# Row blocks of 2560 bytes and seven weight tiles in a one-core decoder step

## The chip, the cores and the metric

The kernel runs on one core of one Trainium2 chip. The metric is the time of one launch in device microseconds (us), the median of several runs.

## The reference

One layer of a decoder on 256 prompt rows and 32 sample rows (eight sequences of four new tokens), 288 rows in all, width 2048, in float32:

```python
def ffn_half(h, g, wg, wu, wd):
    hn = rms_norm(h, g)
    return h + 0.5 * ((jax.nn.silu(hn @ wg) * (hn @ wu)) @ wd)     # inner width 5632
...
hp = ffn_half(hp, norm_ffn1[l], w_ffn1_gate[l], w_ffn1_up[l], w_ffn1_down[l])
cb, u, q, k, v, logf = mixer_in(hp, norm_mix[l], w_in[l], b_f[l])  # one projection, 2048 -> 6152
conv_y = cb * short_conv(u_ext, conv_w[l])                         # half the mixer: gated 3-tap convolution
attn_o = fox_prompt(q, k, v, logf)                                 # the other half: 8 heads of attention
hp = mixer_out(hp, conv_y, attn_o, norm_conv_out[l], norm_attn_out[l], w_out[l])
hp = ffn_half(hp, norm_ffn2[l], w_ffn2_gate[l], w_ffn2_up[l], w_ffn2_down[l])
hp = ple_add(hp, p_prompt[l], norm_ple[l], w_ple_gate[l], w_ple_proj[l])
y_prompt = rms_norm(hp, norm_final)
```

The sample rows go through the same steps; their attention also reads 1024 past tokens per sequence from paged caches of K and V through a page table.

## The kernel before

Features lie on the partitions and the 288 rows along the free axis. A matrix of width 2048 is 16 row blocks of 128 x 288; `h` is the residual stream in this form.

Every product with a weight matrix is taken in three matmuls of one pass each. The rows and the weights are both split into a high part, rounded to the type float32r, and a low part, the remainder. For each row block and each 128 columns of weights, `pair` (its inner `fn`) issues low rows by high weights, high rows by high weights, and high rows by low weights: the first two on L338, the third on L340. The high weights are `whi`, the low ones `wlo`. The first gate and up pairs (`rows_first`) take high before low.

The row operand of most products is `x`, made from `h` by `split` (ScalarE writes the high part, VectorE the low one, L206 and L207). The inner rows of an FFN are `hid`, written in `up` (L417, L418). Both tiles are laid out by `both`: block k has its high part of 288 float32 (1152 bytes), and right behind it its low part, so a block takes 2304 bytes, nine times 256. An offset ahead of the first block (`BEFORE_X` 55 and `BEFORE_W` 7 elements) sets where the parts stand; with the addresses that the allocator gives these tiles, the high parts stand at 252 and the low ones at 124 modulo 256. `zc` (rows of the convolution) and `ph` (per-layer input) are laid out by `both` as well. The attention rows `zah` and `zal` are tiles of their own, at 224 and 96 modulo 256.

Weights come from memory in tiles of four row blocks by 256 columns (512 KB, tags `raw0` to `raw7`, `RAW` = 8). They are loaded by SP's queue in the order of `items`; `load_upto` runs `state["ahead"]` items ahead of use. A tile is split into `whi` and `wlo` in halves of two blocks (L292; ScalarE, then VectorE), five halves ahead of TensorE. A weight tile is free again when its second half is split. The first eight tiles are loaded at the start in smaller parts, interleaved by hand with the parts of `x` (the list `order`); after them SP's queue has the gains and the constants.

During the mixer the V pages (512 KB each, 64 of them) come by indirect DMAs from POOL's queue. In that part only four weight tiles (`WEIGHTS`) serve weights; `page_tile` gives the pages the other weight tiles, three tiles of their own, and one that held attention scores and comes free last:

```python
own = ([(rawp, f"raw{i}") for i in range(WEIGHTS, RAW)] + [(W["vx"][0], f"v{i}") for i in range(VPAGES)]
       + [(W["mix"][0], "wideb")])
n = state["pages"]
state["pages"] += 1
p, tag = own[n] if n < len(own) - 1 else own[(n + 1) % len(own)]
```

Sixteen rounds (`v_round`, four pages and 16 short matmuls each, L825) are set among the products, a round every two or three steps (`VSTEP` 2.7), where a step is one weight tile's matmuls. There `ahead` is 12 items, weights and pages together. Beside page loads, POOL multiplies and adds (masks, residual adds, sums of squares).

The tile framework schedules the instructions of each engine from the order of the program; what is pinned (`keep_in_program_order`) stays in that order.

Of the kernel before, what the change touches and what calls it, by code (L numbers as in the profile page):

```python
# [17 lines left out]
F32R = mybir.dt.float32r  # L18
# [7 lines left out]
P = 128  # L26
D = 2048
KT = D // P
# [4 lines left out]
NT = SEQ + NS  # L33
# [7 lines left out]
NEG = -1e30  # L41
UE = 2 + SEQ + DB * 6

RAW = 8
HALVES = 5
BEFORE_X = 55
BEFORE_W = 7
MANUAL = False
BANKS = dict(mm=3, kt=3, va=2)
KPAIRS = (1, 8, 14, 21, 27, 34, 40, 47)  # L50
# [44 lines left out]
def build(nc, tc, ctx, A, O):  # L95
    def pool(name, bufs=1, to=ctx, **k):
        return to.enter_context(tc.tile_pool(name=name, bufs=bufs, reuse_waits="tile", **k))

    v, s, g, pe, sy = nc.vector, nc.scalar, nc.gpsimd, nc.tensor, nc.sync

    cst = pool("cst")
    xp = pool("xp")
# [96 lines left out]
    def norm_scale(out, squares, width, chunks, load=False):  # L199

        s.activation(sqh, squares, AF.Copy)
        v.tensor_tensor(sql, squares, sqh.bitcast(F32), ALU.subtract)
        defer(lambda: inv_rms(out, [sqh, sql], width, load), chunks)
# [4 lines left out]

    X = {}

    def both(p, name, blocks, before, **k):
        n = blocks * 2 * NT
        whole = 64 if k else 8
        t = p.tile([P, -(-(before + n) // whole) * whole], F32R, name=name, tag=name, **k)
        t = t[:, before:before + n].rearrange("p (k s n) -> p s k n", s=2, n=NT)
        return t[:, 0], t[:, 1]

    def new_x():
        X["hi"], X["lo"] = both(xp, "x", KT, BEFORE_X)

    def make_x(k, gname, work):

        split(X["hi"][:, k, :], X["lo"][:, k, :], h[:, k, :], gain(gname, k))
        squares(k, work)
# [13 lines left out]
    items = []  # L238
    state = dict(wslot=0, pages=0, through=False, ahead=RAW, loaded=0, split=0, used=0, halves_used=0, chunk=0, lead=HALVES)

    def load_upto(n, parts=None):
        while state["loaded"] < min(n, len(items)):
            it = items[state["loaded"]]
            if it["kind"] == "p" and "vx" not in W:
                return
            if it["kind"] == "w":
                state["wslot"] = (state["wslot"] + 1) % (WEIGHTS if state["pages"] and not state["through"] else RAW)
                t = rawp.tile([P, it["nk"], 256], F32, name="wraw", tag=f"raw{state['wslot']}")
                src = it["src"]
                if parts is not None:  # L250
                    cuts = (0, 1, 2, 3, 4) if state["loaded"] < 2 else (0, 2, 4)
                    parts.append([(t[:, a:b], src[:, a:b]) for a, b in zip(cuts, cuts[1:])])
                else:
                    d = sy.dma_start(t, src)
                    if state["used"] < 24:
                        tc.keep_in_program_order(d)
            else:
                t = page_tile()
                g.indirect_dma_start(out=t, out_offset=None, in_=it["src"],  # L259
                                     in_offset=bass.IndirectOffsetOnAxis(ap=it["rows"], axis=0))  # L260
            it["tile"] = t
            state["loaded"] += 1

    def page_tile():
# [6 lines that stand above are left out]
        return p.tile([P, 9 * P] if tag == "wideb" else [P, NH * P], F32, name="page", tag=tag)[:, :NH * P]  # L271
# [85 lines left out]
    def run_steps():  # L357
        for its, _ in steps:
            items.extend(its)
            for it in its:  # L360
                if it["kind"] == "w":
                    halves.extend((it, j) for j in range(0, it["nk"], 2))
        for i in range(0, 16, 4):
            halves[i + 1], halves[i + 2] = halves[i + 2], halves[i + 1]
        for its, fn in steps:
            load_upto(state["used"] + state["ahead"])
            fn()
            state["used"] += len(its)

    def do(fn):  # L370
        steps.append(([], fn))
# [18 lines left out]
    def ffn(wg, wu, wd, nextgain, work):  # L390
        npairs = DFF // 256
        groups = [range(0, 3), range(3, 6)] + [range(p, p + 4) for p in range(6, npairs, 4)]
        H = {}
        for gi, grp in enumerate(groups):
            firstg = gi == 0 and nextgain == "norm_mix"

            def start():
                H["hi"], H["lo"] = both(work(), "hid", 8, BEFORE_W, bufs=2)
            do(start)
            for pi, pr in enumerate(grp):  # L400
                sg = {}

                def gate(b, o, sg=sg):
                    w = work()
                    t = w.tile([P, NT], F32, name="tg", tag="tg", bufs=2)
                    v.tensor_tensor(t, o, rs, ALU.mult)  # L406
                    u = w.tile([P, NT], F32, name="sg", tag="sg", bufs=2)
                    s.activation(u, t, AF.Silu)  # L408
                    r = w.tile([P, NT], F32, name="sr", tag="sr", bufs=3)
                    g.tensor_tensor(r, u, rs, ALU.mult)  # L410
                    sg[b] = r

                def up(b, o, sg=sg, pi=pi):
                    t = work().tile([P, NT], F32, name="hd", tag="hd", bufs=2)
                    v.tensor_tensor(t, o, sg[b], ALU.mult)  # L415
                    k = 2 * pi + b
                    s.activation(H["hi"][:, k, :], t, AF.Copy)  # L417
                    v.tensor_tensor(H["lo"][:, k, :], t, H["hi"][:, k, :].bitcast(F32), ALU.subtract)  # L418

                lead = firstg and pi == 0  # L420
                gs = pair(wg, pr * 256, list(range(KT)), xact, gate, **(dict(late=4 if lead else 2, tag="va", rows_first=lead) if pr == 0 else {}))
                us = pair(wu, pr * 256, list(range(KT)), xact, up, **(dict(late=4, tag="kt", rows_first=True) if lead else {}))
                steps.extend([x for gu in zip(gs, us) for x in gu] if lead else gs + us)
            k0 = grp[0] * 2
            nb = 2 * len(grp)
            lastg = gi == len(groups) - 1
            for ob in range(KT // 2):
                def down(b, o, ob=ob, lastg=lastg):
                    k = 2 * ob + b
                    v.scalar_tensor_tensor(h[:, k, :], o, 0.5, h[:, k, :], ALU.mult, ALU.add)  # L430
                    if lastg:
                        if k == 0:
                            new_x()
                        make_x(k, nextgain, work())
                steps.extend(pair(wd, ob * 256, list(range(k0, k0 + nb)),
                                  lambda k: (H["hi"][:, k, :], H["lo"][:, k, :]), down, k_of=lambda k, k0=k0: k - k0))
        do(lambda: norm_scale(rs, acc, D, 3, True))
# [11 lines left out]
    def x_load(a, b, e=sy):  # L449
        c = slice(KT + a * NT if a else 0, KT + b * NT)  # L450
        tc.keep_in_program_order(e.dma_start(hx[:, c], A["x"][:, c]))
# [67 lines left out]
    for its, _ in steps[2:34]:  # L519
        items.extend(its)  # L520
    first_in = []
    load_upto(8, first_in)
    order = [(0, 1), (s, 0), (sy, 1), (s, 0), (1, 2), (sy, 1), (sy, 0), (sy, 1), (sy, 0), (sy, 1)]
    for a in (2, 3):
        x_load(a, a + 1, g)
    order += [(4, 6), (sy, 2), (sy, 3), (6, 8), (sy, 2), (sy, 3)]
    for a in (4, 6):
        order += [(2 * a, 2 * a + 2), (sy, a), (sy, a + 1), (2 * a + 2, 2 * a + 4), (sy, a), (sy, a + 1)]
    for where, what in order:
        if isinstance(where, int):  # L530
            x_load(where, what)
        else:
            tc.keep_in_program_order(where.dma_start(*first_in[what].pop(0)))
# [388 lines left out]
    def state_in():  # L922
        M["st"] = W["zq"][0].tile([P, CB, DB, 2], F32, name="st")
        M["zc"] = both(W["zq"][0], "zc", CB, BEFORE_W)
        g.dma_start(M["st"].rearrange("p i b t -> p i (b t)"), A["state"])
# [168 lines left out]
    def mix_end():  # L1094
        norm_scale(rs, acc, D, 3)
        state["ahead"] = RAW
        for n in ("vx", "vp", "vv", "cv", "mix", "zq", "tq"):
# [12 lines left out]
    def ple_start():  # L1110
# [4 lines left out]
        g.dma_start(pa, A["p"])  # L1115
        E["hi"], E["lo"] = both(w, "ph", 2, BEFORE_W)
        for k in range(2):
# [61 lines left out]
    do(finish)  # L1179
    with (tc.manual_schedule(engines={mybir.EngineType.PE}) if MANUAL else ExitStack()):  # L1180
        run_steps()
# [67 lines left out]
```

## Time and profile before

| | |
|---|---|
| median of 3 runs | 2266.62 us (2265.76 to 2267.56) |
| the profiled execution's own time | 2266.11 us |
| its span, first to last instruction | 2264.3 us |
| granted TensorE clock | 0.998 |
| TensorE matmul busy | 2250.4 us (99%) |
| VectorE, ScalarE, POOL busy | 1342.5, 1047.3, 323.0 us |
| read from memory | 435.41 MB |

In rows of the profile, "out<-in" names the tiles, the "x" number counts instructions, and what stands behind the bar is busy time, mean ns of one instruction, and idle time of the engine ahead of them with what ended it. In a timeline a row has its start, its length (both in us), the engine and the operation; rows that follow one another with the same names are merged, "x2" being two. In a table of stretches, each row has the stretch, its length, the busy time of TensorE, its weight loads, VectorE, ScalarE and POOL with their counts, the granted clock, the share of time in which the DMA engines were busy, and GB/s. A row of waits has the total, the number of waits and the longest.

### The profile page before, as it was taken

What the parts mean: (1) busy time and instruction counts of PE and PEld (TensorE: products, weight loads), DVE (VectorE), ACT (ScalarE), POOL (GpSimd) and SP (SyncE); (2) the same over time, 40 slices, a digit from 0 to 9 for tenths busy, and PEclk for the clock granted to TensorE, in tenths of its full rate; (3) what the DMA queues carried; (4) which work ended last, traced back from release to release, by engine and by line L of the source; (5) the groups of instructions that cost most, each with busy time, mean ns of one, the idle gap of its engine ahead of it and who ended that gap; (6) DMA issues with size and microseconds to landing.
All of it is one profiled execution on the core that took longest, in us unless ns stands there. A gap on an engine that the chain in (4) does not pass through costs nothing.

```text
span 2264.3 us, 44311 instructions
## 1 busy us (share of the span) xinstructions
PE 2250.4 (99%) x17387; PEld 2194.2 (97%) x17387; DVE 1342.5 (59%) x2413; ACT 1047.3 (46%) x1860; POOL 323.0 (14%) x398
## 2 busy tenths in 40 slices
PE   9999999999999999999999999999999999999997
PEld 9999999999999999888888999999999999999997
DVE  7555555555555586456567875555555555555865
ACT  6444444444444553334344554444444444444654
POOL 1020000000000013345446210000000000000210
PEclk9999999999999999999999999999999999999999
DMA  8575555555555556988988555555555555555552
GB/s 278 169 245 169 170 174 168 168 169 171 172 169 168 168 168 238 332 300 302 331 323 301 167 171 159 179 162 182 168 168 168 174 170 170 168 169 172 169 171 94
DMA packets 342865, 443.37 MB, mean 196 GB/s; under 512 B 17424, under 2 KB 307104, under 8 KB 342656
## 3 DMA queue, kind: packets, MB, share of 16 engines
q1 hardware_dynamic: 320944, 366.25, 50.6%
q0 software_dynamic: 20480, 71.67, 8.9%
q8 instruction: 136, 2.23, 0.4%
q10 hardware_dynamic: 1232, 2.62, 0.3%
q14 instruction: 73, 0.60, 0.1%
HBM read 435.41 MB, written 5.07 MB: 195 GB/s over the span
## 4 chain that ended last, share of the span: by engine, by line
PE 99%; DVE 0%; DMA 0%; issue 0%; ACT 0%; DVEq 0%; ACTq 0%
PE mm L338 61%; PE mm L340 30%; PE va L338 2%; PE va L825 1%; PE va L758 1%; PE va L340 1%; DMA KT<-in_cache_k_dram,idx 0%; PE kt L338 0%; DVE h L1175 0%; PE kt L340 0%; PE kt L879 0%; PE kt L912 0%; PE mm L518 0%; PE kt L903 0%; PE kt L878 0%
## 5 line engine op out<-in xcount | busy, mean ns | idle before, releaser
L338 PE MATMUL mm<-x,whi 128*128 128x288 f32 x7360 | 1438.0, 291 | 0.0
L292 DVE TENSOR_TENSOR wlo<-wraw,whi 128x512 fp32r<-128x512 f32 (+1 forms) x1388 | 974.8, 706 | 748.0 <-ACT whi L292 653.2
L292 ACT ACTIVATE whi<-wraw 128x512 fp32r<-128x512 f32 (+1 forms) x1388 | 862.3, 628 | 881.0 <-PE mm L338 776.9
L338 PEld LDWEIGHTS mm<-x,whi 128*128 128x128 f32 x7360 | 1163.2, 187 | 15.9 <-issue 11.8
L340 PE MATMUL mm<-x,wlo 128*128 128x288 f32 x3680 | 1067.2, 290 | 0.1
L340 PEld LDWEIGHTS mm<-x,wlo 128*128 128x128 f32 x3680 | 689.0, 187 | 0.3 <-DVE wlo L292 0.3
L338 PE MATMUL mm<-hid,whi 128*128 128x288 f32 x2816 | 547.9, 291 | 0.0
L338 PEld LDWEIGHTS mm<-hid,whi 128*128 128x128 f32 x2816 | 445.2, 187 | 0.0
L340 PE MATMUL mm<-hid,wlo 128*128 128x288 f32 x1408 | 408.3, 290 | 0.0
L410 POOL TENSOR_TENSOR sr<-sg,rs 128x288 f32<-128x288 f32 x88 | 71.7, 815 | 1392.8 <-ACT sg L408 1392.6
L340 PEld LDWEIGHTS mm<-hid,wlo 128*128 128x128 f32 x1408 | 263.6, 187 | 0.0
L430 DVE SCALAR_TENSOR_TENSOR h<-mm,h 128x288 f32<-128x288 f32 x192 | 85.8, 454 | 20.0 <-PE mm L340 20.0
L408 ACT ACTIVATE sg<-tg 128x288 f32<-128x288 f32 x88 | 39.0, 444 | 97.7 <-DVE tg L406 97.6
L735 POOL DMA_INDIRECT KT<-in_cache_k_dram,idx x64 | 65.1, 1017 | 129.3 <-DVE idx L166 51.8
L417 ACT ACTIVATE hid<-hd 128x288 fp32r<-128x288 f32 x88 | 39.1, 445 | 92.9 <-DVE hd L415 92.9
L232 POOL TENSOR_TENSOR acc<-acc,sq 128x288 f32<-128x288 f32 x52 | 43.9, 845 | 220.8 <-ACT sq L231 218.3
L259 POOL DMA_INDIRECT page<-in_cache_v_dram,idx x64 | 65.2, 1018 | 63.3 <-PE va L825 42.4
L418 DVE TENSOR_TENSOR hid<-hd,hid 128x288 fp32r<-128x288 f32 x88 | 40.1, 457 | 21.9 <-ACT hid L417 21.9
L338 PE MATMUL mm<-zc,whi 128*128 128x288 f32 x256 | 52.0, 297 | 0.0
L338 PE MATMUL va<-x,whi 128*128 128x288 f32 x256 | 51.2, 293 | 0.0
L415 DVE TENSOR_TENSOR hd<-mm,sr 128x288 f32<-128x288 f32 x86 | 39.0, 454 | 17.1 <-PE mm L340 17.1
L406 DVE TENSOR_TENSOR tg<-mm,rs 128x288 f32<-128x288 f32 x84 | 37.8, 450 | 14.6 <-PE mm L340 13.5
(236 smaller groups left out, 1058.7 us busy)
## 6 DMA issues: line engine op xcount, KB each, us to landing
wraw<-in_w_ffn_gate_dram SPq DMA_DIRECT2D x172, 512.0 KB
wraw<-in_w_ffn_up_dram SPq DMA_DIRECT2D x172, 512.0 KB
wraw<-in_w_ffn_down_dram SPq DMA_DIRECT2D x160, 512.0 KB
wraw<-in_w_in_dram SPq DMA_DIRECT2D x96, 512.0 KB
wraw<-in_w_out_dram SPq DMA_DIRECT2D x32, 512.0 KB
wraw<-in_w_ple_gate_dram SPq DMA_DIRECT2D x32, 512.0 KB
wraw<-in_w_ffn_down_dram SPq DMA_DIRECT2D x32, 256.0 KB
wraw<-in_w_ple_proj_dram SPq DMA_DIRECT2D x8, 256.0 KB
```

The source lines that it names most:

```text
L232: (v if k >= KT - last_on_v else g).tensor_tensor(acc, acc, sq, ALU.add)
L259: g.indirect_dma_start(out=t, out_offset=None, in_=it["src"], in_offset=bass.IndirectOffsetOnAxis(ap=it["rows"], axis=0))
L292: for i in s.activation(hi, x, AF.Copy), v.tensor_tensor(lo, x, hi.bitcast(F32), ALU.subtract):
L338: pe.matmul(o, hi[:, j % 2, w], x, start=f, stop=False)
L340: state["product"] = pe.matmul(o, lo[:, j % 2, w], xh, start=False, stop=l)
L408: s.activation(u, t, AF.Silu)
L410: g.tensor_tensor(r, u, rs, ALU.mult)
L415: v.tensor_tensor(t, o, sg[b], ALU.mult)
L417: s.activation(H["hi"][:, k, :], t, AF.Copy)
L418: v.tensor_tensor(H["lo"][:, k, :], t, H["hi"][:, k, :].bitcast(F32), ALU.subtract)
L430: v.scalar_tensor_tensor(h[:, k, :], o, 0.5, h[:, k, :], ALU.mult, ALU.add)
L735: d = g.indirect_dma_start(out=t[:, i].rearrange("p h s -> p (h s)"), out_offset=None, in_=A["cache_k"], in_offset=bass.IndirectOffsetOnAx ...
```

## The change

A row block of `x` and of `hid` takes 640 elements (2560 bytes, ten times 256) instead of 576, and its low part begins 337 elements (1348 bytes) behind its high part instead of 288. The high parts stay at 252 modulo 256, the low ones go from 124 to 64. `zc` and `ph` keep the old layout. `x` grows by 4096 bytes a partition, the two `hid` tiles together by as much; `RAW` goes from 8 to 7, which gives back 4096. With it the weights run seven items ahead instead of eight, the pages have three weight tiles instead of four, and the start loads seven tiles in the hand-written order; the eighth becomes an ordinary load behind them.

```diff
-RAW = 8
+RAW = 7
...
+FAR = 337
+BLOCK = 640
...
-    def both(p, name, blocks, before, **k):
-        n = blocks * 2 * NT
+    def both(p, name, blocks, before, far=NT, block=2 * NT, **k):
+        n = before + blocks * block
         whole = 64 if k else 8
-        t = p.tile([P, -(-(before + n) // whole) * whole], F32R, name=name, tag=name, **k)
-        t = t[:, before:before + n].rearrange("p (k s n) -> p s k n", s=2, n=NT)
-        return t[:, 0], t[:, 1]
+        t = p.tile([P, -(-n // whole) * whole], F32R, name=name, tag=name, **k)
+        t = t[:, before:n].rearrange("p (k m) -> p k m", m=block)
+        return t[:, :, :NT], t[:, :, far:far + NT]
 
     def new_x():
-        X["hi"], X["lo"] = both(xp, "x", KT, BEFORE_X)
+        X["hi"], X["lo"] = both(xp, "x", KT, BEFORE_X, FAR, BLOCK)
...
-                H["hi"], H["lo"] = both(work(), "hid", 8, BEFORE_W, bufs=2)
+                H["hi"], H["lo"] = both(work(), "hid", 8, BEFORE_W, FAR, BLOCK, bufs=2)
...
-    load_upto(8, first_in)
+    load_upto(RAW, first_in)
...
+    order = [(w, i) for w, i in order if isinstance(w, int) or i < RAW]
```

## The prediction

> **What bounds the kernel now.** I read the page first: span, engine shares, granted clock, and the chain that ended last.
>
> ```profile
> span 2264.3 us, 44311 instructions
> PE 2250.4 (99%) x17387; PEld 2194.2 (97%) x17387; DVE 1342.5 (59%) x2413; ACT 1047.3 (46%) x1860; POOL 323.0 (14%) x398
> PEclk9999999999999999999999999999999999999999
> PE 99%; DVE 0%; DMA 0%; issue 0%; ACT 0%; DVEq 0%; ACTq 0%
> ```
>
> TensorE is on the chain for 99% of the span, with no slice at a reduced clock. VectorE and ScalarE have 41% and 54% of the span to spare. So only two things can move the time: the pace at which one matmul follows another, and a new hole in that stream. The groups of instructions say which matmuls read the tiles that the change moves (x and hid):
>
> ```profile
> L338 PE MATMUL mm<-x,whi 128*128 128x288 f32 x7360 | 1438.0, 291 | 0.0
> L340 PE MATMUL mm<-x,wlo 128*128 128x288 f32 x3680 | 1067.2, 290 | 0.1
> L338 PE MATMUL mm<-hid,whi 128*128 128x288 f32 x2816 | 547.9, 291 | 0.0
> L340 PE MATMUL mm<-hid,wlo 128*128 128x288 f32 x1408 | 408.3, 290 | 0.0
> L338 PE MATMUL va<-x,whi 128*128 128x288 f32 x256 | 51.2, 293 | 0.0
> L340 PE MATMUL va<-x,wlo 128*128 128x288 f32 x128 | 37.5, 293 | 0.0
> L338 PE MATMUL kt<-x,whi 128*128 128x288 f32 x64 | 13.1, 292 | 0.0
> L340 PE MATMUL kt<-x,wlo 128*128 128x288 f32 x32 | 9.5, 297 | 0.0
> ```
>
> The wlo rows (3680, 1408, 128, 32) count one matmul each of a group of three: low rows by whi, high rows by whi, high rows by wlo. That makes 5248 threes. A duration of 291 ns says nothing of the pace, since matmuls overlap; the distance between starts does. Hence the timeline of TensorE in a stretch of the first FFN:
>
> ```profile
> 700.01 0.29 PE L340 MATMUL mm<-x,wlo 128*128 128x288 f32 x1
> ...
> 700.53 0.42 PE L338 MATMUL mm<-x,whi 128*128 128x288 f32 x2
> 700.66 0.29 PE L338 MATMUL mm<-x,whi 128*128 128x288 f32 x1
> 700.79 0.29 PE L340 MATMUL mm<-x,wlo 128*128 128x288 f32 x1
> ...
> 737.34 0.29 PE L340 MATMUL mm<-x,wlo 128*128 128x288 f32 x1
> ```
>
> From 700.01 to 737.34 are 96 threes: 388.9 ns each. Averaged over the 96, a low start is followed by the high start after 130.0 ns, that by the wlo start after 129.8, and that by the next low start after 129.1. 5248 x 0.3889 = 2041 us, 90% of the span, so 1 ns on a three is 5.25 us (0.23%).
>
> **Does the place of a row block matter at all?** The attention rows (zah, zal) have the same shape and the same kind of weights, but other places:
>
> ```profile
> 1266.57 0.29 PE L340 MATMUL mm<-zah,wlo 128*128 128x288 f32 x1
> 1266.70 0.29 PE L338 MATMUL mm<-zal,whi 128*128 128x288 f32 x1
> 1266.83 0.29 PE L338 MATMUL mm<-zah,whi 128*128 128x288 f32 x1
> ...
> 1288.99 0.29 PE L340 MATMUL mm<-zah,wlo 128*128 128x288 f32 x1
> ```
>
> 57 threes in 22.42 us: 393.3 ns, 4.4 more. By steps, again averages of starts: low to high 132.6, high to wlo 131.7, wlo to low 129.0. In the kernel's layout x and hid stand at 252 (high) and 124 (low) modulo 256, zah and zal at 224 and 96; whi stands at 0, wlo at 224. So 28 bytes are worth 4.4 ns. The first pairs show that order matters too. There the same x blocks are taken high, low, high:
>
> ```profile
> 11.32 0.29 PE L340 MATMUL kt<-x,wlo 128*128 128x288 f32 x1
> ...
> 30.59 0.29 PE L340 MATMUL kt<-x,wlo 128*128 128x288 f32 x1
> ```
>
> 49 threes in 19.27 us: 393.3 ns again. So it is the meeting of a row stream with the weight load beside it that costs, and the trace holds two levels, 388.9 and 393.3.
>
> The Trainium skill, "SBUF — State Buffer", section "Who interferes with whom", gives the moving operand and the weight load a read port each, and says that TensorE waits on nobody. By that rule the address would be free, and the sum below would keep only the part of the seven tiles. The zah rows stand against the rule, by 4.4 ns.
>
> **The change part by part.** No instruction is added or removed but for two half-tile loads at the start that become one load; all shapes stay.
>
> *High parts.* They stay at 252 (a block of 2560 bytes is ten times 256), so their place modulo 256, and that of the weights, are as before. Cost 0.
>
> *Low parts, from 124 to 64.* No row of the trace reads 288 columns from 64. Bounds: the fastest step shown is 129.0 ns (wlo to low, in the zah rows), so a three with all steps there takes 387.1: 1.8 less than now, or 5248 x 1.8 = 9.4 us gained. At the other end is the slower level: 4.4 more, 23.1 us lost. Only one matmul in three reads the low part, but the step after it and the step into it have shown that they move with their neighbours. 64 lies further from 124 than 96 does, on the same side, so the nearest row speaks for the slow level; on the other hand a block of 1152 bytes from 64 is 18 whole stretches of 64 bytes, where one from 252, 124, 224 or 96 touches 19, so each start of the trace is a split one and none tells of a whole one. That this counts is a guess; no row shows it. I take the lower end, three steps at the floor: **-9.4 us**, and keep both ends for the range.
>
> *x and hid written with a larger stride.* ScalarE and VectorE write the same 288 contiguous elements. Cost 0: should one of them grow, the idle 41% and 54% of these engines hide it; without that cover it would delay the next row block by its growth.
>
> *Seven tiles in the FFNs and projections.* SP's longest wait is for a free tile:
>
> ```profile
> SPq L254 <- DVE wlo L292: 1390.9, 529, 15.1
> 400.00:600.00 200.00, 200.00 (x1545) 200.00 (x1544) 109.33 (x180) 89.73 (x153) 9.71 (x12) 1.00 0.55 170
> 1040.00:1155.00 115.00, 115.00 (x907) 98.43 (x906) 64.65 (x146) 39.06 (x66) 53.83 (x62) 1.00 0.89 319
> ```
>
> Loads wait for tiles, not matmuls for loads. A tile of four row blocks feeds 24 matmuls, 8 x 0.3889 = 3.1 us, so the store falls from 24.9 to 21.8 us, at a DMA share of 0.55 (second row, before the last number). Cost 0; the cover would have to shrink below a load's own few us.
>
> *The start.* The eighth tile leaves the hand-written order; it now comes behind the gains and the constants, as one load:
>
> ```profile
> 13.42 0.37 SPq L533 DMA_DIRECT2D wraw<-in_w_ffn_up_dram  x1
> 15.51 0.37 SPq L533 DMA_DIRECT2D wraw<-in_w_ffn_up_dram  x1
> 16.87 0.34 SPq L537 DMA_DIRECT2D consts<-in_consts_dram  x1
> 20.56 0.63 ACT L292 ACTIVATE whi<-wraw 128x512 fp32r<-128x512 f32 x1
> 30.72 0.42 PE L338 MATMUL mm<-x,whi 128*128 128x288 f32 x2
> ```
>
> Two issues of 0.7 us leave SP's queue ahead of the constants, so this load goes at about 16.2 us instead of 13.4 and 15.5: 2.8 late for its first half, and the loads queued behind it on SP keep their place. Its first split now runs at 20.56; TensorE wants it 16 threes before 30.72, at 24.4. 2.8 of 3.8 us of slack are used. Cost 0, bounds 0 and +1 us (a gain is excluded: nothing there waits for DMA behind it).
>
> *Page tiles.* The V pages use the weight tiles from the fifth on, so they fall from four to three there, and the whole rotation from eight to seven (six before the last one is free). A page is then loaded into the place of the seventh page before it, at first the sixth. The tight spot is the second round:
>
> ```profile
> 1076.12 1.04 POOL L259 DMA_INDIRECT page<-in_cache_v_dram,idx  x1 [4.35 <-PE va L825]
> 1077.46 0.98 POOL L259 DMA_INDIRECT page<-in_cache_v_dram,idx  x1 [0.30 <-issue]
> 1083.20 1.92 PE L825 MATMUL va<-page,PT 128*32 128x512 f32 x16
> PEld va L825 <- DMA page<-in_cache_v_dram,idx: 0.2, 1, 0.2
> ```
>
> The page issued at 1076.12, when round one had released its place, is used 7.1 us later, with 0.2 us of waiting in the whole kernel. With seven tiles, two pages of round two are released by round one; the second is issued 1.3 us later, so the round starts about 1.3 us late. Later rounds then get their last page as the first of a burst, 7 us ahead, where rounds stand 9 to 14 us apart. POOL stands at such a wait with its later vector work behind it (masks, residual adds), for which VectorE and then the weight splits wait; the splits run five halves ahead. If the scheduler moves other matmuls ahead, nothing is lost. I take **+1.0 us**; bounds 0 and +6 (0.4 us in each of 15 rounds); a gain is excluded, since no transfer becomes shorter.
>
> Sum: -9.4 + 1.0 = -8.4 us against the profiled execution's own 2266.1 us (its span and 1.8 around it): 2257.7. The median of the runs shown, 2266.6, stands 0.5 higher: **2258.2 us**. Its own range is 2254 to 2264.
>
> **Rivals.**
> *The slow level* (the other side): from 64 the low stream meets the weight load as zah and zal do, and a three goes to 393.3. For it: 96 is the nearest row, and two of three known settings are at that level. Against: order alone turned 388.9 into 393.3, so no level belongs to a place by itself. Full price 23.1 + 1.0: 2290.7; it decides from 0.87 ns on a three (4.5 us, 0.2%, about what a measurement here can tell from no change).
> *Nothing in the pace*: the steps stay as they are, and only the pages are left: 2267.6. For it: low and high stand in the same order as before. Against: 28 bytes moved the pace in the zah rows. (The rule on read ports above would end here.)
> *Much faster*: the low matmul loses its whole excess. The prompt's attention reads 256 columns in two passes:
>
> ```profile
> 1173.52 0.59 PE L912 MATMUL kt<-pT,vn 128*128 128x256 f32 x2
> 1173.95 0.38 PE L913 MATMUL kt<-pT,vn 128*128 128x128 f32 x2
> ```
>
> Two of these take 0.43 us, 215 ns for what I take as 512 column times, 0.42 ns each; 288 of them are 121 ns. A low step of 121 instead of 130 gives 5248 x 9 = 47 us: 2220. Against it: no row of 288 columns shows less than 129. The Trainium skill, "TensorE: Matmul & The Clock Gate", section "Back-to-back issue gap", would give N/2.4 + 2.5 = 122.5 ns for 288 columns, an estimate by which this rival would stand at 2228; the traced steps are 6.5 to 11 ns above it.
> *Seven tiles cost more than the pace gives*: POOL's waits reach VectorE and the splits, 10 us or more in the page rounds, with the pace at best a little better: 2273. For it: DMA share 0.89 there (third row of that fence). Against: the same bytes in the same order.
>
> **How the numbers follow.** Forecast 0.43, slow level 0.29, nothing 0.14, much faster 0.09, seven tiles 0.05. The forecast is faster in 0.36 and within 0.2% in 0.07; nothing is within in 0.12, slower in 0.02. Faster 0.36 + 0.09 = 0.45, same 0.19, slower 0.36. The range of 2247 to 2288 leaves out "much faster" and the top of the slow level.
>
> **What would show it.** Starts of TensorE in the FFN: 387 ns a three (right), 393 (slow level), 389 (nothing), 380 (much faster). The three steps apart: the low-to-high one should go from 130.0 to 129. zah rows should stay at 393.3. In the page rounds, waits of PE or PEld for pages should total 1 to 2 us, and POOL's wait for TensorE should exceed before's. At the start, no new hole near 24 us. The forecast is wrong if the threes don't fall below 388.

## The result, and the profile after

The changed kernel takes 2256.32 us (median of 6 runs, 2255.87 to 2257.43); the kernel before, run on the same chip beside it, 2266.70 us (6 runs, 2265.70 to 2270.76). The ratio is 0.9955, with a 95% interval from 0.9945 to 0.9965: 10 us less, 7.9 to 12.5 by the interval. The profiled execution took 2257.17 us, its span is 2255.4, the granted clock 0.998 as before.

The page of the changed kernel, in the same three places as shown of before (span; busy time, share and count of each engine; the chain that ended last):

```profile
span 2255.4 us, 44318 instructions
PE 2240.5 (99%) x17387; PEld 2184.1 (97%) x17387; DVE 1341.1 (59%) x2413; ACT 1046.4 (46%) x1860; POOL 323.0 (14%) x398
PE 98%; DMA 1%; DVE 0%; issue 0%; ACT 0%; SPq 0%; DVEq 0%; POOL 0%; ACTq 0%
```

The same 17387 matmuls, the same bound; TensorE's busy time fell by 9.9 us and the span by 8.9. The groups of matmuls say where (line, names, shapes, count, then busy us and mean ns; the lines have moved down by two):

```profile
L340 PE MATMUL mm<-x,whi 128*128 128x288 f32 x7360 | 1430.5, 291 | 0.0
L342 PE MATMUL mm<-x,wlo 128*128 128x288 f32 x3680 | 1067.4, 290 | 0.1
L340 PE MATMUL mm<-hid,whi 128*128 128x288 f32 x2816 | 544.8, 290 | 0.0
L342 PE MATMUL mm<-hid,wlo 128*128 128x288 f32 x1408 | 408.3, 290 | 0.0
```

Only the whi rows fell, x by 7.5 us and hid by 3.1: these hold the low starts, the only ones whose place was changed. The wlo rows stand where they did. The pace itself is read from a stretch of the first FFN on TensorE's timeline, as before:

```profile
699.85 0.29 PE L342 MATMUL mm<-x,wlo 128*128 128x288 f32 x1
...
700.36 0.42 PE L340 MATMUL mm<-x,whi 128*128 128x288 f32 x2
700.49 0.29 PE L340 MATMUL mm<-x,whi 128*128 128x288 f32 x1
700.62 0.29 PE L342 MATMUL mm<-x,wlo 128*128 128x288 f32 x1
...
737.35 0.29 PE L342 MATMUL mm<-x,wlo 128*128 128x288 f32 x1
```

97 threes in 37.50 us: 386.6 ns each. Averaged over the threes of x and hid outside the first pairs, 388.89 ns became 386.76: 386.67 in undisturbed stretches, and up to some 400 in the few threes behind an interruption. By steps: low to high 130.0 to 128.3, high to wlo 129.7 to 129.2, wlo to low 129.2 and unchanged. A table of stretches shows it for nearly all of the first FFN (stretch, its length, then TensorE's busy time and count, weight loads, VectorE, ScalarE, POOL, clock, DMA share, GB/s). First the kernel before, then the changed one:

```profile
35.00:825.00 790.00, 790.00 (x6095) 789.78 (x6094) 454.74 (x754) 364.87 (x628) 55.42 (x65) 1.00 0.56 175
```

```profile
35.00:825.00 790.00, 790.00 (x6129) 789.77 (x6128) 457.76 (x762) 367.25 (x633) 56.31 (x67) 1.00 0.55 176
```

In the same 790 us, at the same clock, 34 matmuls more: 0.56%, which is 2.2 of 388.9.

What was not touched kept its pace. The attention rows, 61 threes in 24.00 us, and the first pairs, 49 in 19.28 us, are both still at 393.4:

```profile
1263.89 0.29 PE L342 MATMUL mm<-zah,wlo 128*128 128x288 f32 x1
...
1287.89 0.29 PE L342 MATMUL mm<-zah,wlo 128*128 128x288 f32 x1
...
12.20 0.29 PE L342 MATMUL kt<-x,wlo 128*128 128x288 f32 x1
...
31.48 0.29 PE L342 MATMUL kt<-x,wlo 128*128 128x288 f32 x1
```

The sum of the changes: 5184 threes (5248 less 64 in the first pairs) by 2.22 ns would be 11.5 us gained. In the profiled pair, stretch by stretch: 0.9 us is lost at the start, because the first ordinary three begins at 31.61 instead of 30.72. From there to the first matmul on a K page 4.6 us are gained, where its 2184 threes would give 4.9. From that matmul to the first attention row, the part with the pages, it took 381.0 us before and 380.9 after: 0.1 gained of the 1.4 that 632 threes would give. Behind it 5.1 are gained of 5.3 (2368 threes). Together that is 8.9, the difference of the spans.

### The profile page after: what moved, and what is told of

It reads as the page before. It is cut to its first block, busy times and chain, and to the rows that moved or that the text cites. A ratio compares the mean times of both kernels' runs of the same rounds, so it can differ in the third digit from the quotient of the medians.

```text
span 2255.4 us, 44318 instructions
## 1 busy us (share of the span) xinstructions
PE 2240.5 (99%) x17387; PEld 2184.1 (97%) x17387; DVE 1341.1 (59%) x2413; ACT 1046.4 (46%) x1860; POOL 323.0 (14%) x398
## 4 chain that ended last, share of the span: by engine, by line
PE 98%; DMA 1%; DVE 0%; issue 0%; ACT 0%; SPq 0%; DVEq 0%; POOL 0%; ACTq 0%
PE mm L340 61%; PE mm L342 31%; PE va L340 1%; PE va L828 1%; PE va L761 1%; PE va L342 1%; DMA KT<-in_cache_k_dram,idx 0%; PE kt L340 0%; DMA page<-in_cache_v_dram,idx 0%; DVE h L1178 0%; DMA h<-in_x_dram 0%; PE kt L342 0%; PE kt L882 0%; PE kt L915 0%; PE kt L906 0%
## 5 line engine op out<-in xcount | busy, mean ns | idle before, releaser
L261 POOL DMA_INDIRECT page<-in_cache_v_dram,idx x64 | 65.8, 1028 | 66.4 <-PE va L828 43.7
```

## The experiments

Except where said otherwise, each kernel is the changed one with the edit shown; a "place" is a byte address modulo 256. Where a kernel was run once, that is said; there the levels of the pace are the result, not the time.

**Which part of the change: the seven tiles, the stride, or the place?** The first kernel is the old layout with seven tiles:

```diff
-FAR = 337
-BLOCK = 640
+FAR = 288
+BLOCK = 576
```

> The layout of before (blocks of 2304 bytes, low parts at 124) with seven weight tiles. Theory A (the gain is the low part's place, the seven tiles cost a little in the page rounds): threes stay at 388.9 ns, the time is 1 to 2 us above before, about 2267.7 us. Rival B (fewer tiles give part of the gain, by loads that run less far ahead): below 2265 us. Rival C (the seven tiles cost several us, and the layout alone is worth more than the 11.6 us that its threes show): above 2270 us.

Measured: 2268.11 us (11 runs) beside 2267.56 for the kernel before; ratio 1.0002, interval 0.9992 to 1.0011, so between 1.8 us gained and 2.5 lost. The seven tiles alone cost nothing that can be measured. In the second, blocks take 2560 bytes and the parts lie apart as in the change, but the low part is back at 124:

```diff
-FAR = 337
+FAR = 352
```

> Blocks of 2560 bytes and seven tiles as in the changed kernel, but the low parts 352 elements behind the high ones, so at 124 modulo 256 as before. Theory A (the place modulo 256 decides): threes of 388.9 ns, the time of the kernel with seven tiles alone, about 2267.7 us. Rival D (the longer block or the gap between high and low decides, whatever the place): threes of 386.7 ns, about 2256.3 us.

Measured: 2267.94 us, ratio 1.0003 (0.9994 to 1.0012). The threes of the two, in the same stretch of the timeline as above, first the seven tiles alone, then the larger stride:

```profile
699.85 0.29 PE L342 MATMUL mm<-x,wlo 128*128 128x288 f32 x1
...
737.57 0.29 PE L342 MATMUL mm<-x,wlo 128*128 128x288 f32 x1
```

```profile
699.91 0.29 PE L342 MATMUL mm<-x,wlo 128*128 128x288 f32 x1
...
737.64 0.29 PE L342 MATMUL mm<-x,wlo 128*128 128x288 f32 x1
```

97 threes in 37.72 and 37.73 us: 388.9 in both. The whole gain comes with the low parts' place.

**What is it about 64?** Two kernels give each of the twelve groups of inner rows (two FFNs, six groups each) another place. In the first the high part stays at 252 and the low part moves, in the second the low part stays at 64 and the high one moves:

```diff
+PLACES = [(7, 337), (7, 288), (7, 321), (7, 329), (7, 336), (7, 338), ...]
...
-                H["hi"], H["lo"] = both(work(), "hid", 8, BEFORE_W, FAR, BLOCK, bufs=2)
+                H["hi"], H["lo"] = both(work(), "hid", 8, *PLACES.pop(0), BLOCK, bufs=2)
```

> The changed kernel, but the inner rows of the twelve FFN groups have their low parts, in order of the groups, at 64, 124, 0, 32, 60, 68, 80, 96, 128, 160, 192, 224 modulo 256, with the high parts always at 252. Read from the threes of hid in each group. Theory A1 (a low part that starts on a multiple of 64 touches 18 stretches of 64 bytes and is the fast one): 386.7 ns at 64, 0, 128 and 192, 388.9 or more at the others, 60 and 68 among them. Theory A2 (64 is one spot of a pattern over 256 bytes set by where the weight load stands): 64 fast, 0, 128 and 192 differ from it and from one another; 124 gives 388.9 in both; 96 gives up to 393.3. The whole time stays within 3 us of the changed kernel's.

> The changed kernel, but the inner rows of the twelve FFN groups have their high parts, in order of the groups, at 252, 0, 32, 60, 64, 96, 124, 128, 160, 188, 192, 224 modulo 256, with the low parts always at 64. Theory A1 (whole stretches of 64 bytes are fast): high parts at 0, 64, 128, 192 give threes under 386.7 ns, since two of three matmuls read the high part. Theory A2 (a pattern over 256 bytes): no such common gain; 252 is among the fastest, some places reach 393 ns.

Measured, as averages over the 95 or 127 threes of one group (ns):

| low part at (high at 252) | 64 | 0 | 124 | 32, 60, 80, 96, 128 | 192 | 68, 224 | 160 |
|---|---|---|---|---|---|---|---|
| three | 386.7 | 386.7 | 388.9 | 393.3 | 395.6 | 396.7 | 400.0 |

| high part at (low at 64) | 252 | 0, 32, 60, 64, 124, 128, 188, 192 | 160, 224 | 96 |
|---|---|---|---|---|
| three | 386.7 | 393.3 to 393.4 | 397.8 | 399.8 |

The ends of three groups on the first kernel's timeline: low at 0 (97 threes in 37.51 us, 386.7), at 68 (96 in 38.08, 396.7), at 160 (95 in 38.00, 400.0):

```profile
331.85 0.29 PE L343 MATMUL mm<-hid,wlo 128*128 128x288 f32 x1
...
369.36 0.29 PE L343 MATMUL mm<-hid,wlo 128*128 128x288 f32 x1
...
779.89 0.29 PE L343 MATMUL mm<-hid,wlo 128*128 128x288 f32 x1
...
817.97 0.29 PE L343 MATMUL mm<-hid,wlo 128*128 128x288 f32 x1
...
1794.83 0.29 PE L343 MATMUL mm<-hid,wlo 128*128 128x288 f32 x1
...
1832.83 0.29 PE L343 MATMUL mm<-hid,wlo 128*128 128x288 f32 x1
```

That the good places are multiples of 64, and with it the guess of the prediction that eighteen whole stretches of 64 bytes count, falls: 128 and 192 are such starts too and lie at 393.3 and 395.6, and a low part four bytes behind 64 costs 396.7. The whole times, 2266.94 and 2267.95 (one run each), are near that of the kernel before; that of the first was expected within 3 us of the changed kernel's and missed it by 10.6, since more places than expected are dear. x, at 252 and 64 throughout, came back to 386.7 after every dear group, so each group was entered from there.

**The place that looked as good, used everywhere; and the other order.** Low parts of x and hid at 0:

```diff
-FAR = 337
+FAR = 321
```

> The changed kernel with every low part of x and hid at 0 modulo 256 (321 elements behind the high one) instead of 64. The group of hid with its low parts at 0 had threes of 386.7 ns, made up otherwise (126.7, 131.0 and 129.0 ns). Theory A2 (the sum of a three is set by where the four operands stand to one another): 386.7 ns throughout and the changed kernel's time, 2256 to 2257 us. Rival (the result for hid doesn't carry over to x, or the steps' other split costs somewhere): above 2260 us.

Measured: 2273.37 us (7 runs, 2272.55 to 2275.13) beside 2266.47, ratio 1.0030 (1.0018 to 1.0041): slower than the kernel before, where 2256 was expected. The timeline, again from wlo starts of x, in the first FFN and then in the second:

```profile
699.99 0.29 PE L342 MATMUL mm<-x,wlo 128*128 128x288 f32 x1
...
737.50 0.29 PE L342 MATMUL mm<-x,wlo 128*128 128x288 f32 x1
...
1850.01 0.29 PE L342 MATMUL mm<-x,wlo 128*128 128x288 f32 x1
...
1887.77 0.29 PE L342 MATMUL mm<-x,wlo 128*128 128x288 f32 x1
```

97 threes in 37.51 us (386.7), then 96 in 37.76 (393.3), from the same tile at the same place. In the first FFN x and hid run at 386.7 throughout, in the mixer the pace changes between the two levels at interruptions, and from the attention rows on (about 1313 us) it stays at 393.3 through the whole second FFN. So a stream with the low part at 0 has two levels and stays in the one it falls into. The sweep had met this place only coming from 386.7 and so showed the better one alone.

The other order, low part at 64 as in the change but high, low, high in every product:

```diff
-                        for x in (xh, xl) if rows_first else (xl, xh):
+                        for x in (xh, xl):
```

> The changed kernel with all threes taken in the order high, low, high (as the first pairs are) instead of low, high, high; same matmuls, places and weights. Theory A2 with the meeting of row stream and weight load: 393.3 ns a three, as in the first pairs, so 5184 x 6.67 = 34.6 us above the changed kernel, about 2291 us. Rival (a three's cost belongs to the places of the rows alone): 386.7 ns in either order, about 2256 us, and the first pairs are slow for another reason.

Measured: 2274.62 us (one run); neither theory. The same two stretches:

```profile
699.99 0.29 PE L342 MATMUL mm<-x,wlo 128*128 128x288 f32 x1
...
737.50 0.29 PE L342 MATMUL mm<-x,wlo 128*128 128x288 f32 x1
...
1849.91 0.29 PE L342 MATMUL mm<-x,wlo 128*128 128x288 f32 x1
...
1887.67 0.29 PE L342 MATMUL mm<-x,wlo 128*128 128x288 f32 x1
```

386.7 again, then 393.3 (96 threes in 37.76 us). At 252 and 64, then, the order does not set the price; with it this pair of places, too, stays at the level it falls into. At other places the order does cost. The attention rows of the same kernel, at 224 and 96, take 60 threes in 24.00 us, 400.0 ns where low, high, high took 393.3:

```profile
1266.42 0.29 PE L342 MATMUL mm<-zah,wlo 128*128 128x288 f32 x1
...
1290.42 0.29 PE L342 MATMUL mm<-zah,wlo 128*128 128x288 f32 x1
```

The convolution's rows, at 252 and 124, go from 388.9 to 393.6 on average.

**Is a level carried over from what ran before?** Two kernels, one place each, tell the history of the stream from the place of its own tile: x at 0 with hid at 64, and x at 64 with hid at 0:

```diff
-        X["hi"], X["lo"] = both(xp, "x", KT, BEFORE_X, FAR, BLOCK)
+        X["hi"], X["lo"] = both(xp, "x", KT, BEFORE_X, 321, BLOCK)
```

```diff
-                H["hi"], H["lo"] = both(work(), "hid", 8, BEFORE_W, FAR, BLOCK, bufs=2)
+                H["hi"], H["lo"] = both(work(), "hid", 8, BEFORE_W, 321, BLOCK, bufs=2)
```

> The changed kernel with the low parts of x at 0 and those of hid left at 64. Theory H (at 0 a stream of threes can run at 386.7 or at 393.3 ns, whichever it falls into, and keeps it; at 64 it always comes back to 386.7): after the attention rows x runs at 393.3 ns until the first inner rows of the second FFN, which bring the stream to 386.7, and from there x and hid stay at 386.7 to the end of that FFN. The time is then about 12 us under that of the kernel with both at 0 (2273.4), so about 2261 us. Rival P (the second x tile or the second FFN is slow at 0 for a reason of its place): x stays at 393.3 ns in the whole second FFN, hid at 386.7, about 2265 us.

> The changed kernel with the low parts of hid at 0 and those of x left at 64. Theory H: x enters every group of inner rows at 386.7 ns, hid at 0 keeps what it meets, so all twelve groups run at 386.7 ns and the time is the changed kernel's, about 2256 us. Rival P (place in the second FFN): hid at 393.3 ns in the six groups of the second FFN, 4.7 us more, about 2261 us.

Measured: 2260.62 and 2256.86 us (one run each; the kernel before beside them 2265.67). The first kernel's timeline, x after the attention rows, then the first hid of the second FFN, then x again:

```profile
1349.71 0.29 PE L342 MATMUL mm<-x,wlo 128*128 128x288 f32 x1
...
1388.26 0.29 PE L342 MATMUL mm<-x,wlo 128*128 128x288 f32 x1
...
1394.86 0.29 PE L342 MATMUL mm<-hid,wlo 128*128 128x288 f32 x1
...
1425.80 0.29 PE L342 MATMUL mm<-hid,wlo 128*128 128x288 f32 x1
...
1849.97 0.29 PE L342 MATMUL mm<-x,wlo 128*128 128x288 f32 x1
...
1887.48 0.29 PE L342 MATMUL mm<-x,wlo 128*128 128x288 f32 x1
```

98 threes in 38.55 us (393.4); 80 in 30.94 (386.8); 97 in 37.51 (386.7). x at 0 comes out of the attention rows at 393.4, the rows at 64 bring the stream down within about 1 us, and x at 0 then stays at 386.7 to the end of the FFN. The second kernel, hid at 0 in the second FFN, 97 threes in 37.50 us:

```profile
1789.85 0.29 PE L342 MATMUL mm<-hid,wlo 128*128 128x288 f32 x1
...
1827.35 0.29 PE L342 MATMUL mm<-hid,wlo 128*128 128x288 f32 x1
```

All twelve groups at 0 run at 386.7, since x at 64 leads into each. That the level is carried over is shown; a level that belongs to the tile's place alone would have kept hid at 393.3 in the second FFN, as in the kernel with both at 0.

**More pairs of places, and the weights' own.** The edit of the sweeps with other pairs (high, low):

```diff
+PLACES = [(7, 337), (7, 322), (7, 333), (7, 335), (7, 349), (7, 320), (6, 338), (6, 337), ...]
```

> The changed kernel, but hid stands, group by group, with (high, low) at (252,64), (252,4), (252,48), (252,56), (252,112), (252,252), (248,64), (248,60), (124,0), (128,0), (0,128), (188,60) modulo 256. Theory A2 with narrow good spots: 386.7 ns at (252,64) alone or at few others, 393 ns and more at most. Rival (only the distance from high to low counts): (248,60), (188,0-like shifts) and (0,64-like shifts) with a distance of 68 bytes are as good as (252,64); here (248,60) and (252,64) are equal.

Measured (one run, 2266.57 us): 386.7 for (252, 64) alone. (252, 56) 390.0; (252, 112) and (188, 60) 391.1; (252, 4), (252, 48), (252, 252) and (128, 0) 393.3 to 393.4; (248, 60) and (124, 0) 396.7; (248, 64) 397.9; (0, 128) 400.0. The good place at (252, 64) is a spot a few bytes wide, and it is not the distance of the two parts: (248, 60) has that of (252, 64) and costs 10 ns more.

The last kernel moves the weights as well, by group, in tiles that are 64 elements longer; for room there are six weight tiles:

```diff
-RAW = 7
+RAW = 6
...
-            hi = wsp.tile([P, 2, 256], F32R, name="whi", tag="whi")
-            lo = wlp.tile([P, 2, 256], F32R, name="wlo", tag="wlo")
+            hi, lo = (p.tile([P, 576], F32R, name=n, tag=n)[:, o:o + 512].rearrange("p (k c) -> p k c", c=256)
+                      for p, n, o in ((wsp, "whi", it["where"][0]), (wlp, "wlo", it["where"][1])))
```

> Six weight tiles, and weights and inner rows moved group by group. (high, low; high weights, low weights) modulo 256: (252,64;0,224) as in the changed kernel, then all four moved by 32, by 64, by 128 and by 4, then low weights at 0, 32, 64, 128, 192, then high weights at 64 and 128. x stays at (252,64). Theory A2 (places to one another): hid keeps 386.7 ns where all four are moved together, and changes where weights are moved alone. Rival (the absolute place of the rows counts, weights don't): hid's threes change when all are moved together, and stay at 386.7 ns when only weights are moved.

Measured (one run, 2282.21 us): whi, wlo and both parts of hid moved together by 32, 64 or 128 bytes keep 386.7 (up to 386.8 on average, with a few slower threes on entry), moved together by 4 they go to 397.9. With hid left at 252 and 64, moving wlo alone by 32 or 96 gives 386.7 and by 64, 160 or 224 gives 393.3; moving whi alone by 64 or 128 gives 393.3. From the timeline, all four by 128 (98 threes in 37.89 us, 386.6) and all four by 4 (95 in 37.80, 397.9):

```profile
484.72 0.29 PE L344 MATMUL mm<-hid,wlo 128*128 128x288 f32 x1
...
522.61 0.29 PE L344 MATMUL mm<-hid,wlo 128*128 128x288 f32 x1
...
635.06 0.30 PE L344 MATMUL mm<-hid,wlo 128*128 128x288 f32 x1
...
672.86 0.29 PE L344 MATMUL mm<-hid,wlo 128*128 128x288 f32 x1
```

A group's moved weights also serve its gate and up products, whose rows, x, stay at 252 and 64. Coming from hid at 386.7 to 386.8, x went to 393.3 where both weights were moved by 32, by 128 or by 4, and where wlo alone was moved by 160; both moved by 64 left it at 386.7. The first of these, 96 threes in 37.76 us:

```profile
119.38 0.29 PE L344 MATMUL mm<-x,wlo 128*128 128x288 f32 x1
...
157.14 0.29 PE L344 MATMUL mm<-x,wlo 128*128 128x288 f32 x1
```

So it is the place of the rows against that of the weights that counts, and something finer than 32 bytes besides. Four settings (wlo alone by 64 or 224, whi alone by 64 or 128) were entered at 393.3 and stayed there; whether they would also leave 386.7 is not shown, only that they don't come back to it as the places of the changed kernel do. With six tiles the pages are no longer free: from the first page to the last it takes 181.6 us instead of 174.8, with 4.9 us of waiting for pages.

## Why the prediction was right, step by step

**The low parts' place** (-9.4 us by the prediction). The mechanism is shown: both kernels with the place undone give the gain back, 2268.11 and 2267.94. The size was too small by a fifth, 9.4 us of 11.5. The term took 129.0 ns as the fastest step and three such steps as the end; but 129.0 was only the fastest step at the old places. At 64 the low-to-high step is 128.3, and with the low part at 0 it was 126.7 (with 131.0 and 129.0 behind it: steps trade time with each other, only the sum of three is a level). The three is 386.67, not 387.1, and 5184 of them would gain 11.5 us. The count was 64 too high, the first pairs, which stayed at 393.

The choice between the two bounds was right, its reason was not: that 64 came out at the good end was luck. The guess that 64 gives whole stretches of 64 bytes fell with 128 and 192. The warning from the nearest row, 96, was sound as a measure of risk: of the twelve low places of the first sweep two reached 386.7, one 388.9, and nine cost 393.3 or more, and of the five more tried later with the high part at 252 none came below 390.0.

**"Order matters too"** is right at the old places: the convolution's rows, at 252 and 124 like x then, go from 388.9 to 393.6 when only the order changes. At 252 and 64 it is half right. The first pairs at 393.3, and the second FFN of the high-first kernel, show high, low, high at the upper level; its first FFN shows the same order and places at 386.7. There the order takes away the return to the lower level and does not set one.

**The stride of x and hid** (0): the kernel with the larger stride and the low part at 124 is within its interval of no change.

**Seven tiles in the FFNs** (0): right, as far as 1.8 to 2.5 us can tell.

**The start** (0, at most +1). The first ordinary three stands 0.9 us later than before, but not for the reason feared: TensorE's wait is at the very beginning. Rows of TensorE and ScalarE on the timeline, with what ended the wait in brackets:

```profile
7.58 0.65 PE L340 MATMUL va<-x,whi 128*128 128x288 f32 x2 [0.81 <-ACT whi L294]
6.69 0.53 ACT L208 ACTIVATE x<-h 128x288 fp32r<-128x288 f32 x1 [2.19 <-DMA h<-in_x_dram]
```

ScalarE waited 2.19 us for the first load of x, 1.00 in the profiled execution before, long ahead of the eighth tile's load; and with the same seven tiles the first ordinary three stands at 31.34 in the old layout and at 30.62 with the larger stride. It scatters by that much from execution to execution, so none of it is put down to the change.

**The pages** (+1.0). The total of waits came out (1.2 us, where 1 to 2 was named as the sign), the place of it did not. Round two was to begin 1.3 us late. Its second page is indeed issued behind the first, as the prediction said, but it lands in time (POOL's issues, then TensorE's round):

```profile
1071.15 1.04 POOL L261 DMA_INDIRECT page<-in_cache_v_dram,idx  x1 [4.44 <-PE va L828]
1072.49 0.98 POOL L261 DMA_INDIRECT page<-in_cache_v_dram,idx  x1 [0.30 <-issue]
1078.22 1.96 PE L828 MATMUL va<-page,PT 128*32 128x512 f32 x16
...
1089.61 3.06 PE L828 MATMUL va<-page,PT 128*32 128x512 f32 x16
...
1102.77 1.92 PE L828 MATMUL va<-page,PT 128*32 128x512 f32 x16
```

Round two starts 9.26 us after round one, 9.27 before: a page used 5.7 us after its issue is not late. The failed step is the one that made an issue 1.3 us later into a round 1.3 us later, without the slack of that load. The wait stands in round three instead, which takes 3.06 us where others take 1.92:

```profile
PEld va L828 <- DMA page<-in_cache_v_dram,idx: 1.0, 1, 1.0
```

Against 0.2 before, 0.6 with seven tiles alone, 1.4 with the larger stride. POOL's wait for TensorE ahead of a page rose from 42.4 to 43.7 us, the direction foretold. From the first page to the last the three kernels with seven tiles take 175.5 to 176.3 us against 174.8, and in the two that run at 388.9 the part before it, with the K pages, 0.8 to 1.5 less, so that the whole is even. Eight tiles with the new layout were not run.

**The rivals.** The slow level did not come, but it lies beside: of the eleven other low places five are at 393.3 and four above, and so is the high-first order in part of the kernel. "Nothing in the pace" falls with 386.7 against 388.9. It was also where the Trainium skill would have ended, "SBUF — State Buffer", section "Who interferes with whom": independent read ports for the moving operand and the weight load, TensorE waiting on nobody. The runs disagree: x at the same places goes from 386.7 to 393.3 when both weight tiles are moved by 32 bytes, or wlo alone by 160. "Much faster" falls: in no stretch of any run did a step of 288 columns average less than 125.7 ns (x with both weight tiles moved by 64), and the steps beside it were longer, so that no level of a three came below 386.67. "Seven tiles cost more" falls with the kernel that has them alone.

## What to carry to other kernels

When TensorE is the bound and every matmul brings its own weights, the place of the rows against the weights modulo 256 is worth up to 3.4% (386.7 to 400.0 ns a three here), and it can be tried by shifting a tile, with no instruction changed. A sweep in short stretches can mislead: a place must be tried over the whole kernel, coming out of a disturbance, because some streams keep the level they fall into. To read so small a change, take distances between starts over a hundred repeats; the mean duration of a matmul (290 or 291) hides it.

## What the runs showed of the hardware that was not expected

The pace of a three is not continuous. Nearly all levels seen lie whole steps of 2.22 ns above 386.67: 388.89 (one step), 391.1 (two), 393.33 (three), 395.5 (four), 397.8 (five), 400.0 (six); 390.0 and 396.7 lie halfway.

At (252, 0) and, in the order high, low, high, at (252, 64), there are two levels, 386.67 and 393.33, and the stream keeps either for hundreds of microseconds. Even the first pairs, high, low, high in every kernel, show it: with x at (252, 64) they run at 393.3 in the changed kernel and at 386.7 in the one with the high parts moved, though the two programs are the same up to there. But at (252, 64) in the order low, high, high the stream returned to 386.67 after every disturbance shown, within about 1 us. That is what makes the change worth 10 us where the place 0, equally fast at its best, is 7 us slower than the kernel before. What inside the chip sets the levels, and why moving everything by 4 bytes costs 11 ns a three and by 32 nothing, stays open.

A further version was not run: the first pairs taken low first (64 threes by 6.67 ns, 0.4 us) and the attention, convolution and per-layer rows at the good places (about 1.2 us by their counts) would bring some 1.6 us by this estimate, 0.07%, less than these runs can tell.
